# Row sums of a 16384 x 1024 array: a first load from the last group of rows, in place of a first block of 17 rows a partition

## The chip, the cores and the metric

The kernel runs on one core of one Trainium2 chip. The metric is the time of one execution on the device in microseconds (us), as the median of several runs. One further execution is taken with the hardware profiler; all durations of single instructions come from it.

## What is computed

```python
def setup_inputs():
    batch, seq, dim = 32, 512, 1024
    return {"x": np.random.randn(batch, seq, dim).astype(np.float32)}

def reference(x):
    return np.sum(x, axis=-1).astype(np.float32)
```

16384 rows of 1024 float32 are summed: 67.1 MB are read from HBM and 64 KB are written.

## The kernel before

**Tiles and loads.** The 16384 rows are shared out over 128 partitions, 128 rows each. The list `sizes` cuts them into eight blocks of 17, 15 and six times 16 rows a partition; within a block, partition p holds that many consecutive rows of `x`. So one partition's part of a load is a contiguous run, and neighbouring partitions begin 17, 15 or 16 rows (68, 60 or 64 KB) apart. `rows_from(j, n)` gives the n rows from the j-th on.

All loads are issued by SP, in program order, into tiles of the pool `in`, which has three buffers: a tile can be loaded anew once the sums of what it held are done. `rows(t, a, n, j, n_act, pairs)` (L208) issues one load of n rows a partition into tile `t` from place `a` on, and gives the sums of the last `n_act` of them to ScalarE (ACT) and of the others to VectorE (DVE).

**The three ways to sum a row.**
- `vec` (L172): one VectorE reduction over all its rows of the load at once.
- `halves` (L186), used with `pairs=True`: one VectorE instruction a row, which adds the two halves of the row and accumulates the result, and then a short read of the accumulator.
- `act` (L199): one ScalarE copy a row into PSUM with an accumulated sum, and a read of the accumulator. Its PSUM pool has four buffers, so each copy waits for the fourth before it, on the same engine.

All sums go into one SBUF tile, `sums`, 128 partitions x 128.

**The order of the loads.** Block 0 is loaded as 4 rows (`FIRST`) and 13 rows; then block 1 (15 rows) and blocks 2 to 6 (16 rows each). Block 6 is summed half by ACT, half by VectorE. The last block comes as 8 rows, 5 rows, 2 rows and one row in two pieces of 560 and 464 elements (L247, L248), so that little is left to sum when the last bytes arrive. The two pieces of the last row are summed by two `halves`; the first one's sum is put beside the second piece as a further element, and a small copy (`seen`) makes the second wait for it. The load of block 1 is held (`hold`, L230) until the first 4 rows are summed, and so are, behind it on SP, all the loads that follow.

**The stores.** On ACT's queue, behind its last copy and held until the load of 2 rows has landed, stand three stores: the sums of block 0 (17 a partition), of block 1 (15 a partition), and of blocks 2 to 6 (L252 for the first two, L254 for the third). The sums of the last block are stored by SP (L260).

**What is done to the finished program.** `issue_first_load_at_entry` moves the very first load in front of the meeting of all engines with which a program begins. `order_waits` puts, of several waits of one instruction, a given one first. `wait_for_the_store_at_the_clear` changes the end of the program (its instructions carry L286): there SP waits for everything that is still under way, all engines meet, GpSimd (POOL) clears the semaphores, and all meet again. The wait for SP's own last store is taken out of SP's waits and put behind POOL's clears, right before the last release; SP's waits for the ACT stores stay where they are.

Of the kernel before, what the change touches and what calls it, by code (L numbers as in the profile page):

```python
# [118 lines left out]
@with_exitstack  # L119
def kernel(  # L120
    ctx: ExitStack,
    tc: tile.TileContext,
    x: bass.AP,
    out: bass.AP,
):
    nc = tc.nc
    nc.at_finalize(issue_first_load_at_entry)
    nc.at_finalize(order_waits)
    nc.at_finalize(wait_for_the_store_at_the_clear)
    fp32 = mybir.dt.float32  # L130
    P = 128
    batch, seq, dim = x.shape
    rows = batch * seq
    J = rows // P
    BIG = 16

    sizes = [BIG + 1, BIG - 1] + [BIG] * (J // BIG - 2)  # L140
    begins = [sum(sizes[:k]) for k in range(len(sizes))]
    x_r = x.flatten_outer_dims()
    out_r = out.rearrange("b s -> (b s)")
    x_b = [
        x_r[a * P : (a + n) * P].rearrange("(p j) d -> p j d", p=P) for a, n in zip(begins, sizes)
    ]
    out_b = [out_r[a * P : (a + n) * P].rearrange("(p j) -> p j", p=P) for a, n in zip(begins, sizes)]
    out_g = out_r[2 * BIG * P :].rearrange("(g p j) -> p g j", p=P, j=BIG)

    def rows_from(j, n):  # L150
        k = max(k for k, a in enumerate(begins) if a <= j)
        j -= begins[k]
        return x_b[k][:, j : j + n, :]

    last = J // BIG - 1
    FIRST = 4
    pieces = (560, 464)

    with (
        tc.tile_pool(name="in", bufs=3) as inpool,
        tc.tile_pool(name="unread", bufs=4, space=bass.MemoryType.PSUM) as upool,
        tc.tile_pool(name="stage", bufs=1) as stpool,
        tc.manual_schedule(),
    ):
        sums = stpool.tile([P, J], fp32)
        seen = stpool.tile([P, 1], fp32)
        scratch = stpool.tile([P, pieces[1] // 2 + 1], fp32)

        def vec(dst, src):
            return nc.vector.tensor_reduce(  # L172
                out=dst, in_=src, axis=mybir.AxisListType.X, op=mybir.AluOpType.add
            )

        def hold(inst, until, reason):
            tc.add_manual_dep(
                inst.ins,
                until.ins.name,
                mybir.DependencyInfo(mybir.DependencyClass.Sync, mybir.DependencyReason.DATA),  # L180
                reason=reason,
            )

        def halves(dst, src, unread=None):
            n = src.shape[-1] // 2
            return nc.vector.tensor_tensor_reduce(  # L186
                out=src[:, :n] if unread is None else unread[:, :n],
                in0=src[:, :n],
                in1=src[:, n:],
                scale=1.0,  # L190
                scalar=0.0,
                op0=mybir.AluOpType.add,
                op1=mybir.AluOpType.add,
                accum_out=dst,
            )

        def act(dst, src, n):
            unread = upool.tile([P, dim], fp32)
            nc.scalar.activation(  # L199
                out=unread[:, :n],  # L200
                in_=src,
                func=mybir.ActivationFunctionType.Copy,
                accum_out=dst,
            )

        sums_of = []

        def rows(t, a, n, j, n_act, pairs=False):  # L208
            nv = n - n_act
            block = t[:, a * dim : (a + n) * dim].rearrange("p (n d) -> p n d", d=dim)  # L210
            load = nc.sync.dma_start(out=block, in_=rows_from(j, n))  # L211
            if pairs:
                for q in range(nv):
                    sums_of.append(halves(sums[:, j + q : j + q + 1], block[:, q, :]))
            else:
                sums_of.append(vec(sums[:, j : j + nv], block[:, :nv, :]))
            for q in range(nv, n):
                act(sums[:, j + q : j + q + 1], block[:, q, :], dim)
            return load

        for g in range(last):
            n, j = sizes[g], begins[g]
            t = inpool.tile([P, (BIG + 1) * dim], fp32)
            if g == 0:
                rows(t, 0, FIRST, j, 0)
                first = sums_of[-1]
                rows(t, FIRST, n - FIRST, j + FIRST, 0)
                continue
            load = rows(t, 0, n, j, BIG // 2 if g == last - 1 else 0)
            if g == 1:  # L230
                hold(load, first, "no descriptors of later loads while the first ones start")

        t = inpool.tile([P, (BIG + 1) * dim], fp32)
        j = last * BIG
        rows(t, 0, 8, j, 4)
        rows(t, 8, 5, j + 8, 2, pairs=True)
        two = rows(t, 13, 2, j + 13, 1, pairs=True)
        a = BIG - 1

        j += a
        c, width = pieces
        whole = t[:, a * dim + c : BIG * dim + 2]
        nc.vector.memset(whole[:, width + 1 :], 0.0)  # L245
        part = t[:, a * dim : a * dim + c]
        nc.sync.dma_start(out=part, in_=rows_from(j, 1)[:, 0, :c])  # L247
        nc.sync.dma_start(out=whole[:, 1 : width + 1], in_=rows_from(j, 1)[:, 0, c:])  # L248
        behind = "its packets come behind those of the loads"
        for k in range(2):  # L250
            mine = sums[:, begins[k] : begins[k] + sizes[k]]
            hold(nc.scalar.dma_start(out=out_b[k], in_=mine), two, behind)  # L252
        middle = sums[:, 2 * BIG : last * BIG].rearrange("p (g j) -> p g j", j=BIG)
        hold(nc.scalar.dma_start(out=out_g[:, : last - 2], in_=middle), two, behind)  # L254
        halves(whole[:, :1], part)


        nc.vector.tensor_copy(out=seen, in_=whole[:, :1])  # L258
        halves(sums[:, j : j + 1], whole, unread=scratch)
        nc.sync.dma_start(out=out_b[last], in_=sums[:, last * BIG :])  # L260


# [28 lines left out]
```

## Time and profile before

| | |
|---|---|
| time, median of 3 runs | 162.37 us (162.19 to 162.58) |
| time of the profiled execution | 162.19 us |
| its span in the profile | 160.33 us |
| loads, mean over the span | 419 GB/s |
| VectorE busy | 120.2 us |
| ScalarE busy | 17.3 us |
| packets of the stores from ACT's queue (q10) | 944 |

The span runs from the first to the last instruction of the program that the profiler saw; 1.86 us of the execution's time lie around it. Lines such as L172 are lines of the kernel above; SPq and ACTq are the queues on which SP and ACT issue transfers. In the list of the issues, the columns are the tensor written and read, the issuing engine, how many, the size, and the microseconds from issue to landing. In the other views, the last figures of an instruction's line are its shortest, median and longest duration in ns and the start of its first and last one in us.

### The profile page before, as it was taken

The page shows a single profiled execution, that of the slowest core. Times are in us where ns is not written, and L with a number is a line of the kernel's source. Part 1 is how long each engine was busy: PE and PEld are TensorE (multiplying, and loading weights), DVE is VectorE, ACT ScalarE, POOL GpSimd, SP SyncE. Part 2 cuts the span into 40 slices and gives each one's busy share as a digit, 9 for nine tenths or more (in the row PEclk, how much of TensorE's full clock was granted, in tenths as well). Part 3 has the DMA queues.
Part 4 walks back from the last instruction along what each step waited for, and adds up shares of the span by engine and source line. Part 5 has one row for each costly group of instructions (what it writes and reads, how often), then busy time and mean ns, then how long its engine had stood idle before and what let it go on. Part 6 is the DMA issues. An engine that isn't in the chain of part 4 may idle for free.

```text
span 160.3 us, 130 instructions
## 1 busy us (share of the span) xinstructions
DVE 120.2 (75%) x23; ACT 17.3 (11%) x31; POOL 0.2 (0%) x4
## 2 busy tenths in 40 slices
DVE  0190029992699938999499994999949999597944
ACT  3000000000000000000000000000000000596952
POOL 0000000000000000000000000000000000000000
DMA  7999999997996996997997998999969969999993
GB/s 258 478 425 425 425 458 491 491 399 337 523 507 278 523 507 278 523 458 327 523 441 343 523 425 360 523 392 392 523 294 491 523 278 507 392 392 430 414 400 81
DMA packets 2960, 67.18 MB, mean 419 GB/s; under 512 B 1296, under 2 KB 1424, under 8 KB 1552
## 3 DMA queue, kind: packets, MB, share of 16 engines
q1 hardware_dynamic: 2016, 67.12, 97.4%
q10 hardware_dynamic: 944, 0.06, 0.4%
HBM read 67.11 MB, written 0.07 MB: 419 GB/s over the span
## 4 chain that ended last, share of the span: by engine, by line
DMA 73%; DVE 24%; SPq 1%; issue 0%; DVEq 0%
DMA t<-in_x_dram 73%; DVE sums L172 24%; SPq L211 1%; DVE t L186 0%; DVE scratch L186 0%; DVE seen L258 0%; DVEq L286 0%
## 5 line engine op out<-in xcount | busy, mean ns | idle before, releaser
L172 DVE TENSOR_REDUCE sums<-t 128x16 f32<-128x16384 f32 (+4 forms) x9 | 116.6, 12954 | 35.6 <-DMA t<-in_x_dram 35.6
L199 ACT ACTIVATE unread<-t 128x1024 f32<-128x1024 f32 x15 | 15.2, 1012 | 139.5 <-DMA t<-in_x_dram 139.5
L186 DVE CUSTOM_DVE_ANT_0 t<-t 128x512 f32<-128x512 f32 (+1 forms) x5 | 3.1, 642 | 2.3 <-DMA t<-in_x_dram 2.3
L199 ACT ACTIVATION_READ_ACCUMULATOR unread<-t 128x1 f32 x15 | 2.8, 187 | 0.0
L199 ACT ACT_TABLE_LOAD x1 | 1.3, 1283 | 0.8 <-PEq L275 0.8
L186 DVE DVE_READ_ACCUMULATOR2_ANT sums<- 128x1 f32 x5 | 0.4, 83 | 0.0
L186 DVE CUSTOM_DVE_ANT_0 scratch<-t 128x233 f32<-128x233 f32 x1 | 0.4, 403 | 0.0
L258 DVE COPY seen<-t 128x1 f32<-128x1 f32 x1 | 0.2, 154 | 0.0
L275 POOL MEMSET const-bfloat16-1.0<- 128x1 bf16 x1 | 0.1, 101 | 0.0
L275 POOL MEMSET const-uint8-127<- 128x1 uint8 x1 | 0.1, 101 | 0.0
L275 POOL MEMSET const-float32-0.0<- 128x1 f32 x1 | 0.1, 98 | 0.2 <-issue 0.2
L275 POOL MEMSET const-float32-1.0<- 128x1 f32 x1 | 0.1, 98 | 0.0
L186 DVE DVE_READ_ACCUMULATOR2_ANT t<- 128x1 f32 x1 | 0.1, 83 | 0.0
L245 DVE MEMSET t<- 128x1 f32 x1 | 0.1, 59 | 0.0
## 6 DMA issues: line engine op xcount, KB each, us to landing
t<-in_x_dram SPq DMA_DIRECT2D x1, 7680.0 KB, 29.4
t<-in_x_dram SPq DMA_DIRECT2D x1, 6656.0 KB, 22.4
t<-in_x_dram SPq DMA_DIRECT2D x1, 4096.0 KB, 31.1
t<-in_x_dram SPq DMA_DIRECT2D x1, 2560.0 KB, 36.9
t<-in_x_dram SPq DMA_DIRECT2D x1, 2048.0 KB, 7.4
t<-in_x_dram SPq DMA_DIRECT2D x1, 1024.0 KB, 38.9
t<-in_x_dram SPq DMA_DIRECT2D x1, 280.0 KB, 39.2
t<-in_x_dram SPq DMA_DIRECT2D x1, 232.0 KB, 39.2
```

Of the source, the lines that this page charges most:

```text
L172: return nc.vector.tensor_reduce(out=dst, in_=src, axis=mybir.AxisListType.X, op=mybir.AluOpType.add)
L186: return nc.vector.tensor_tensor_reduce(out=src[:, :n] if unread is None else unread[:, :n], in0=src[:, :n], in1=src[:, n:], scale=1.0, sc ...
L199: nc.scalar.activation(out=unread[:, :n], in_=src, func=mybir.ActivationFunctionType.Copy, accum_out=dst,)
L211: load = nc.sync.dma_start(out=block, in_=rows_from(j, n))
L245: nc.vector.memset(whole[:, width + 1 :], 0.0)
L258: nc.vector.tensor_copy(out=seen, in_=whole[:, :1])
L275: nc = _bacc.Bacc("TRN2", target_bir_lowering=False, num_devices=1)
```

## The change

The blocks of 17 and 15 rows go; there are eight groups of 16 rows a partition, all 64 KB apart from partition to partition. The first load is now of seven rows of the last group (`FIRST = 7`), into a tile of its own, summed by one reduction. Then seven whole groups are loaded by one load each. The last of these is summed by VectorE as nine single rows (`pairs=True`) and by ACT as seven. Then the remaining nine rows of the last group follow as 6 rows (four on VectorE, two on ACT), 2 rows (one each) and the same two pieces of one row. The load of group 1 is held until the first seven rows are summed. The three stores from ACT become one, of the sums of groups 0 to 6, held as they were until the load of 2 rows has landed. What is done to the finished program is the same.

```diff
-    sizes = [BIG + 1, BIG - 1] + [BIG] * (J // BIG - 2)
-    begins = [sum(sizes[:k]) for k in range(len(sizes))]
-    x_r = x.flatten_outer_dims()
-    out_r = out.rearrange("b s -> (b s)")
-    x_b = [
-        x_r[a * P : (a + n) * P].rearrange("(p j) d -> p j d", p=P) for a, n in zip(begins, sizes)
-    ]
-    out_b = [out_r[a * P : (a + n) * P].rearrange("(p j) -> p j", p=P) for a, n in zip(begins, sizes)]
-    out_g = out_r[2 * BIG * P :].rearrange("(g p j) -> p g j", p=P, j=BIG)
+    x_g = x.flatten_outer_dims().rearrange("(g p j) d -> g p j d", p=P, j=BIG)
+    out_v = out.rearrange("b s -> (b s)").rearrange("(g p j) -> p g j", p=P, j=BIG)
 
     def rows_from(j, n):
-        k = max(k for k, a in enumerate(begins) if a <= j)
-        j -= begins[k]
-        return x_b[k][:, j : j + n, :]
+        return x_g[j // BIG, :, j % BIG : j % BIG + n, :]
...
-    FIRST = 4
+    FIRST = 7
...
+        def store(eng, g0, g1):
+            return eng.dma_start(
+                out=out_v[:, g0:g1],
+                in_=sums[:, g0 * BIG : g1 * BIG].rearrange("p (g j) -> p g j", j=BIG),
+            )
+        j = last * BIG
+        t = inpool.tile([P, BIG * dim + 4], fp32)
+        rows(t, 0, FIRST, j, 0)
+        first = sums_of[-1]
         for g in range(last):
-            n, j = sizes[g], begins[g]
-            t = inpool.tile([P, (BIG + 1) * dim], fp32)
-            if g == 0:
-                rows(t, 0, FIRST, j, 0)
-                first = sums_of[-1]
-                rows(t, FIRST, n - FIRST, j + FIRST, 0)
-                continue
-            load = rows(t, 0, n, j, BIG // 2 if g == last - 1 else 0)
+            t = inpool.tile([P, BIG * dim + 4], fp32)
+            if g < last - 1:
+                load = rows(t, 0, BIG, g * BIG, 0)
+            else:
+                rows(t, 0, BIG, g * BIG, 7, pairs=True)
             if g == 1:
                 hold(load, first, "no descriptors of later loads while the first ones start")
 
-        t = inpool.tile([P, (BIG + 1) * dim], fp32)
-        j = last * BIG
-        rows(t, 0, 8, j, 4)
-        rows(t, 8, 5, j + 8, 2, pairs=True)
-        two = rows(t, 13, 2, j + 13, 1, pairs=True)
+        t = inpool.tile([P, BIG * dim + 4], fp32)
+        rows(t, FIRST, 6, j + FIRST, 2, pairs=True)
+        two = rows(t, FIRST + 6, 2, j + FIRST + 6, 1, pairs=True)
         a = BIG - 1
...
-        behind = "its packets come behind those of the loads"
-        for k in range(2):
-            mine = sums[:, begins[k] : begins[k] + sizes[k]]
-            hold(nc.scalar.dma_start(out=out_b[k], in_=mine), two, behind)
-        middle = sums[:, 2 * BIG : last * BIG].rearrange("p (g j) -> p g j", j=BIG)
-        hold(nc.scalar.dma_start(out=out_g[:, : last - 2], in_=middle), two, behind)
+        hold(store(nc.scalar, 0, last), two, "its packets come behind those of the loads")
         halves(whole[:, :1], part)
...
-        nc.sync.dma_start(out=out_b[last], in_=sums[:, last * BIG :])
+        store(nc.sync, last, last + 1)
```

## The prediction

> **What bounds the kernel now.** I read the page's shares first, then the queues, then the chain of waits. Each fence below is one view.
>
> ```profile
> DVE 120.2 (75%) x23; ACT 17.3 (11%) x31; POOL 0.2 (0%) x4
> ...
> q1 hardware_dynamic: 2016, 67.12, 97.4%
> ```
>
> No compute engine is near full, while the load queue q1 keeps the 16 DMA engines busy for 97.4% of the span: the kernel is one stream of loads with a start before it and an end behind it. The chain in order of time shows where the stream stops deciding:
>
> ```profile
> 117.98 39.15 DMA t<-in_x_dram
> 157.13 0.03 issue
> 157.16 0.47 DVE t L186 x2
> 157.63 0.02 issue
> 157.65 0.15 DVE seen L258
> 157.80 0.33 DVE scratch L186
> 158.13 0.01 DVEq L286
> ```
>
> The stream (but for its last piece) is in at 157.13 and VectorE ends at 158.13, yet the span is 160.3. So 2.2 us lie behind the last arithmetic. For these I read the issues of the stores, SP's own waits, and the end sequence (L286) cut into two windows, 158.5 to 159.45 and 159.9 to 160.33:
>
> ```profile
> out_dram<-sums ACTq DMA_DIRECT2D x1, 40.0 KB, 1.9
> out_dram<-sums ACTq DMA_DIRECT2D x1, 8.5 KB, 1.5
> ...
> out_dram<-sums SPq DMA_DIRECT2D x1, 8.0 KB, 1.4
> ```
> ```profile
> SPq L286 <- DMA out_dram<-sums: 0.7, 1, 0.7
> ```
> ```profile
> L286 SPq EVENT_SEMAPHORE x4: 28/28/678, 158.6 to 159.4; - x4
> ```
> ```profile
> L286 POOLq EVENT_SEMAPHORE x3: 17/17/17, 159.9 to 160.3; - x3
> ```
>
> The timeline puts the four stores' issues at 156.48 and, 0.49 later, 156.97 (ACT, 17 and 15 sums a partition), at 157.40 (ACT, 40 KB) and at 158.16 (SP, the last 8 KB):
>
> ```profile
> 157.40 0.44 ACTq L254 DMA_DIRECT2D out_dram<-sums  x1
> ...
> 158.16 0.35 SPq L260 DMA_DIRECT2D out_dram<-sums  x1
> ```
>
> The 40 KB store lands at about 157.40 + 1.95 = 159.35, the last one at 158.16 + 1.42 = 159.58. SP stands 678 ns on the former, until 159.37. The rest of the end (two meetings of all engines, two semaphore clears) then takes from 159.37 to 160.33, 0.96 us, and the last store is waited for only in POOL's wait near 160.2, where it has been in for 0.6 us. **So the end is set by the third ACT store, not by the last store**, and the three waits of 17 ns in the last fence show that nothing else is waited for there.
>
> **The change, part by part.**
>
> *The loads.* Starts of the VectorE reductions follow landings by 0.02 us: 7.45, 23.16, 41.32, 60.66, 80.01, 99.37, 118.71, 138.07, 147.78, 153.92, 156.42. The gaps are 15.71 us for 13 rows, 18.16 for 15, 19.35 for 16, 9.71 for 8, 6.14 for 5, 2.50 for 2. A line through 16 and 2 rows is (19.35 - 2.50) / 14 = 1.204 us a row and 0.093 a load; it gives 15.74, 18.15, 9.72 and 6.11 for the others. The first load of 4 rows lands at 7.43, 2.52 more than its 4.91 by that line. The new loads are 7, seven times 16, 6, 2 and the two pieces, 12 in place of 13, so the stream ends 0.09 earlier: 7 rows at 7.45 + 3 x 1.204 = 11.06, the seventh group at 11.06 + 7 x 19.35 = 146.51, 6 rows (7.32) at 153.83, 2 rows at 156.33, against 156.42.
>
> *Buffers and SP's queue.* The load of the second group waits for the first reduction, which at 8.69 / 8 = 1.08 us a row takes 7.6 us and ends at 18.6 (before: 11.87). Behind it on SP stand all later loads. The queue holds 7 + 16 rows until 30.4, so nothing runs dry; without the whole group behind the first load it would cost 18.6 - 11.0 = 7.6 us. Each later load waits for the reduction two groups before the landing one: group 3 for the reduction of group 0, 30.4 + 17.2 = 47.6, with group 2 queued until 69.1. The four last loads wait for group 4 (107.8 + 17.2 = 125.0) with group 6 queued until 146.5. Over 20 us of cover each time; SP issues in 0.33 to 0.46 us each.
>
> *VectorE and ACT at the tail.* Group 6 gives VectorE 9 rows as pairs (0.615 us a row, from 153.92, 154.54, 155.15) in place of 8 at 1.08: done by 146.5 + 5.6 = 152.1, before the 6 rows come at 153.83. ACT does 7 rows in 7.4 us (8 took 8.4): 153.9, 0.1 behind the 6 rows. Its two rows end at 156.0, before 156.33: free. VectorE now has 4 rows there where it had 3: 153.83 + 4 x 0.615 + 0.08 = 156.37, 0.04 after the landing of the 2 rows. So of the 0.09 gained, 0.05 reach the last reduction, which ends at 158.08, and the last store is issued at 158.11. Each further 0.1 of delay on VectorE there would move the end by 0.1.
>
> *The stores.* Two ACT issues of 0.39 us go. One store of 7 groups, 7 x 128 runs of 64 B, waits for the 2 rows, for VectorE's and ACT's sums of group 6 (152.1 and 153.9, long past), and is issued where the first was, 0.06 behind the landing: about 156.4. Behind it on ACT stands only the end. No row shows such a store. 128 runs took 1.5, 640 took 1.9, so 512 more cost 0.4 and 896 should take 2.1: landed at 158.5. The far bound is 1.9 x 896 / 640 = 2.7: 159.1. SP comes to its end waits at 158.56 - 0.05 = 158.5 and to the next ones every 0.07, so at 2.1 the store holds it for 0.07 at most, against 0.68. I take 2.1, since both rows show a large fixed part. Then POOL comes to its last wait 0.66 to 0.7 earlier, near 159.55, and now meets the last store's landing at 158.11 + 1.42 = 159.53. Both bounds agree: the end moves from 160.33 to about 159.65, **0.68 earlier, of which 0.05 comes from the loads and 0.63 from the store**.
>
> *The start.* Before, partition p of the first block begins 17 rows (68 KB) after its neighbour, the second block 15 rows; now every load has a pitch of 64 KB, and the first one starts all DMA engines from rest at that pitch. No row has this. In the running stream the pitch costs nothing: 15.71 / 13 = 1.208 us a row at 68 KB against 19.35 / 16 = 1.209 at 64 KB. From rest, the first load's 2.52 us hold 0.9 before the first packet and a slow first packet on each engine: 1.1 us on the mean of the stretch from 0.9 to 2.0 (18.9 us of engine time for 17 packets), against 0.61 for the following ones. The low bound is a gain of 0.1 (larger packets). The high bound is that the first packet, now 28 KB or 1.07 us long, takes twice as long on the last engine: +1.07. I take 0, by the row of the same pitch.
>
> A rule speaks against this part. The Trainium skill, "DMA: Bandwidth & Descriptors", section "Latency and other measured facts", reports that copies whose partitions lie a large power of two apart lose rate (207 GB/s at 512 KiB, 103 at 4 MiB, 214 again with 4 KiB of padding), and its cause there is only inferred. The trace agrees so far as it goes that 64 KB apart is harmless while the stream runs. By the rule's mildest case, an estimate from that page, the first load would lose 3%, about 0.3 us of its 8.5, and the sum would be a gain of 0.4 in place of 0.7.
>
> *Sum.* The profiled execution took 162.19 for a span of 160.33. 162.19 - 0.68 = 161.51. It is the lowest of the three runs, 0.18 under the median, so the median becomes 162.37 - 0.68 = **161.7**.
>
> **The rivals.** 0.2% is about what a measurement of this kernel can tell from no change: 0.32 us.
>
> 1. *The start at 64 KB pitch loses more than the end gains.* For it: the first packets are the only ones in the trace that run slower than the ports, so the engines do collide at the start, and the engines' first rows now lie whole multiples of 64 KB apart. Against it: the issue itself spreads the first packets over 0.9 to 1.9 us. The whole stream would shift, since nothing later can catch up with it. Price at its bound: -0.68 + 1.07 = +0.39, 162.8. It decides for slower from 1.0 us of extra start; a second packet as slow would give 163.8.
> 2. *The start takes back about half.* A loss of 0.36 to 1.0 leaves -0.32 to +0.32; at 0.6, 162.3.
> 3. *The merged store is slow.* At the far bound it lands at 159.1, SP leaves its wait at 159.13, and as this wait now stands one place earlier in the row, 0.07 + 0.96 follow: 160.16, a gain of 0.17, 162.2. For it: 896 runs in one issue. Against it: the fixed 1.4 us of the 8 KB store.
> 4. *The end gains, but less, because the last store lands late,* in the 1.5 to 1.7 of the small ACT stores: the gain is 0.4 to 0.6, still faster, 161.9. It is part of the forecast's own range, 161.4 to 162.0.
>
> **How the numbers follow.** Faster by 0.68 or somewhat less: 0.48. Rival 1: 0.34, since the bound is only a guess from one packet and no row shows the start. Rivals 2 and 3 together: 0.18. These are the chances of faster, slower and the same. The time is the likeliest one, 161.7. The range goes down to 161.3 (0.1 gained at the start, the other 0.3 run-to-run: the three runs spread over 0.39) and up to 162.9, just past rival 1's bound; beyond that is left perhaps 0.15.
>
> **What would show it.** Right: the first reduction starts near 11.06 and the first whole group's near 30.4; groups 19.35 apart; the 2 rows' reduction near 156.37; one ACT store of 56 KB landing in about 2.1; no long wait of SP on a store in the end; POOL's clears near 159.3. Rival 1 shows as a first reduction at 12 or later, with all starts behind it shifted as much and groups still 19.35 apart. Rival 3 shows as a landing over 2.5 and SP's wait on it. The prediction is wrong if the groups' distance grows beyond 19.35: then the pitch costs in the stream too, and seven groups multiply it.

## The result and the profile after

| | before | after |
|---|---|---|
| median of 6 runs each | 162.33 us (162.13 to 162.58) | 161.58 us (161.40 to 161.66) |
| profiled execution | 162.19 us | 161.59 us |
| its span | 160.33 us | 159.7 us |

The ratio is 0.9952, with a 95% interval of 0.9940 to 0.9965: 0.75 us less on the medians, 0.60 in the two profiled executions. The prediction was 161.7, by a gain of 0.68.

The page of the changed kernel, its share of the load queue:

```profile
q1 hardware_dynamic: 1872, 67.12, 97.7%
```

Its timeline, the landings as VectorE sees them (start and length in us, line, tiles, then the idle time before it and what ended it):

```profile
11.07 7.62 DVE L161 TENSOR_REDUCE sums<-t 128x7 f32<-128x7168 f32 x1 [11.07 <-DMA t<-in_x_dram]
30.40 17.22 DVE L161 TENSOR_REDUCE sums<-t 128x16 f32<-128x16384 f32 x1 [11.71 <-DMA t<-in_x_dram]
...
127.18 17.22 DVE L161 TENSOR_REDUCE sums<-t 128x16 f32<-128x16384 f32 x1 [2.14 <-DMA t<-in_x_dram]
...
146.62 0.69 DVE L175 CUSTOM_DVE_ANT_0 t<-t 128x512 f32<-128x512 f32 x1 [2.23 <-DMA t<-in_x_dram]
...
156.41 0.69 DVE L175 CUSTOM_DVE_ANT_0 t<-t 128x512 f32<-128x512 f32 x1
156.50 0.41 ACTq L211 DMA_DIRECT2D out_dram<-sums  x1
...
157.16 0.45 DVE L175 CUSTOM_DVE_ANT_0 t<-t 128x280 f32<-128x280 f32 x1
...
158.17 0.35 SPq L211 DMA_DIRECT2D out_dram<-sums  x1
```

The last store is issued at 158.17, where it was issued before at 158.16. Up to there the two executions are level: the loads gave nothing in this one. The gain lies in what follows. Its issues of stores (size in KB, us to landing) and SP's own waits:

```profile
out_dram<-sums ACTq DMA_DIRECT2D x1, 56.0 KB, 2.1
out_dram<-sums SPq DMA_DIRECT2D x1, 8.0 KB, 1.4
```
```profile
SPq L200 <- DMA t<-in_x_dram: 17.9, 5, 10.9
SPq L276 <- PEq L276: 0.7, 2, 0.5
```

The row of SP waiting 0.7 us for `out_dram<-sums` is gone; the row on PEq, one of the meetings, was there before with the same numbers. The end sequence between 158.5 and 159.45, and from the kernel before the clears of POOL, in the window from 159.9 to 160.33:

```profile
L276 SPq EVENT_SEMAPHORE  x5: 17/28/28, 158.6 to 159.1; - x5
...
L276 POOLq EVENT_SEMAPHORE_RANGE_CLEAR  x2: 46/58/71, 159.3 to 159.4; - x2
```
```profile
L286 POOLq EVENT_SEMAPHORE_RANGE_CLEAR  x2: 44/59/74, 160.0 to 160.1; - x2
```

None of SP's semaphore instructions there is longer than 28 ns, where one was 678, and POOL clears at 159.3 to 159.4, where it cleared at 160.0 to 160.1. The one ACT store, issued at 156.50, landed at 158.63, just before SP came to its wait at 158.65. The last store landed at 159.60, and POOL's last wait, which is for it, ended 0.02 us later; before, that store had been in for 0.64 us by then.

### The profile page after: what moved, and what is told of

It reads as the page before. It is cut to its first block, busy times and chain, and to the rows that moved or that the text cites. A ratio compares the mean times of both kernels' runs of the same rounds, so it can differ in the third digit from the quotient of the medians.

```text
span 159.7 us, 134 instructions
## 1 busy us (share of the span) xinstructions
DVE 120.7 (76%) x41; ACT 11.9 (7%) x21; POOL 0.2 (0%) x4
## 4 chain that ended last, share of the span: by engine, by line
DMA 71%; DVE 27%; SPq 0%; issue 0%; DVEq 0%
DMA t<-in_x_dram 71%; DVE sums L161 26%; SPq L200 0%; DVE t L175 0%; DVE scratch L175 0%; DVE seen L248 0%; DVEq L276 0%
## 5 line engine op out<-in xcount | busy, mean ns | idle before, releaser
L161 DVE TENSOR_REDUCE sums<-t 128x16 f32<-128x16384 f32 (+1 forms) x7 | 110.9, 15848 | 33.5 <-DMA t<-in_x_dram 33.5
L188 ACT ACTIVATE unread<-t 128x1024 f32<-128x1024 f32 x10 | 10.1, 1013 | 144.9 <-DMA t<-in_x_dram 144.9
L175 DVE CUSTOM_DVE_ANT_0 t<-t 128x512 f32<-128x512 f32 (+1 forms) x15 | 9.2, 672 | 4.0 <-DMA t<-in_x_dram 3.9
L188 ACT ACTIVATION_READ_ACCUMULATOR unread<-t 128x1 f32 x10 | 1.9, 187 | 0.0
L175 DVE DVE_READ_ACCUMULATOR2_ANT sums<- 128x1 f32 x15 | 1.2, 82 | 0.0
```

What stands on the lines that cost most here:

```text
L161: return nc.vector.tensor_reduce(out=dst, in_=src, axis=mybir.AxisListType.X, op=mybir.AluOpType.add)
L175: return nc.vector.tensor_tensor_reduce(out=src[:, :n] if unread is None else unread[:, :n], in0=src[:, :n], in1=src[:, n:], scale=1.0, sc ...
L188: nc.scalar.activation(out=unread[:, :n], in_=src, func=mybir.ActivationFunctionType.Copy, accum_out=dst,)
```

## The experiments

Each was timed in five or more runs beside the kernel before on the same chip; "before" is that median. The profile quoted is of one execution. "Store theory" in the expectations is the reading of the prediction: the end waits for the last of the ACT stores.

**Three stores again, in the changed kernel.**

```diff
-        hold(store(nc.scalar, 0, last), two, "its packets come behind those of the loads")
+        for g0, g1 in ((0, 1), (1, 2), (2, last)):
+            hold(store(nc.scalar, g0, g1), two, "its packets come behind those of the loads")
```

> The changed kernel with its one ACT store split again into groups 0, 1 and 2 to 6. Store theory: the third store is issued 0.9 us after the first and lands near 159.35, SP stands on it for about 0.65 us, and the time goes back by 0.6, to 162.2, level with the kernel before. Rival, that the gain lies in the loads: the time stays at 161.6.

Measured 162.20 against 162.25 before, ratio 1.0003 (0.9995 to 1.0012). With its loads untouched, the changed kernel has lost the whole gain. SP's waits and ACT's issues there:

```profile
SPq L277 <- DMA out_dram<-sums: 0.7, 1, 0.7
```
```profile
156.35 0.91 ACTq L211 DMA_DIRECT2D out_dram<-sums  x2
...
157.35 0.39 ACTq L211 DMA_DIRECT2D out_dram<-sums  x1
...
158.03 0.35 SPq L211 DMA_DIRECT2D out_dram<-sums  x1
```

The wait is back, and the third issue comes 1.0 us after the first.

**Two stores, in the changed kernel.** The same edit with `((0, 1), (1, last))`.

> The changed kernel with its ACT store as two, of group 0 and of groups 1 to 6. Store theory, in which the end follows the landing of the last ACT store: the second is issued 0.49 after the first and lands 2.1 later, near 159.1; SP comes to its wait for it near 158.65 to 158.7, stands 0.35 to 0.45 us, and the time is 161.9 to 162.0, between one store (161.6) and three (162.2). Rival, that only the number of runs or bytes in flight counts: 161.6, as with one.

Measured 161.85 against 162.22, ratio 0.9982 (0.9973 to 0.9991), between the other two. SP's wait:

```profile
SPq L277 <- DMA out_dram<-sums: 0.4, 1, 0.4
```

So one, two and three stores give waits of 0, 0.4 and 0.7 us and times of 161.6, 161.85 and 162.2. The time follows the wait, not the bytes, which are the same each time. The step from one to two costs less than the wait: 0.25 on the medians, and 0.36 if one counts from the issue of the last store to the end of the span (1.92 against 1.57 us). With one store POOL waits some 0.04 us for the last store instead; the rest of the difference lies in the streams.

**The small stores early, in the kernel before.** The loads stay as they were; the stores of blocks 0 and 1 are moved out of the tail.

```diff
+            if g == 4:
+                for k in range(2):
+                    nc.scalar.dma_start(out=out_b[k], in_=sums[:, begins[k] : begins[k] + sizes[k]])
...
-        for k in range(2):
-            mine = sums[:, begins[k] : begins[k] + sizes[k]]
-            hold(nc.scalar.dma_start(out=out_b[k], in_=mine), two, behind)
```

(The semaphore of the last store comes to lie at the edge of the cleared range, so that POOL needs one clear there, not two. This brings nothing: POOL's last wait ends 0.02 us after the landing of the last store here too.)

> The kernel before with its loads untouched (17, 15 and 16 rows, first load of 4), but the stores of blocks 0 and 1 issued by ACT as soon as their sums are done, near 57 us, long before its copies; only the 40 KB store stays behind the 2-row load. Store theory: it is issued 0.9 earlier, lands at 158.4 to 158.5, SP does not wait for it, and the time falls by 0.5 to 0.7, to 161.6 to 161.8; the 256 small runs cost the stream at most 16 x 0.01 = 0.16 us. Rival, that the loads of the change bring the gain: 162.3.

Measured 161.66 against 162.22, ratio 0.9968 (0.9956 to 0.9980). This is the gain of the change with none of its loads: the changed kernel measured 161.60 on the same chip. The two small stores went out at 37.26 and 57.54. The wait of SP on a store is gone from its profile, and the early stores show something else:

```profile
out_dram<-sums ACTq DMA_DIRECT2D x1, 40.0 KB, 1.9
out_dram<-sums ACTq DMA_DIRECT2D x1, 8.5 KB, 23.7
out_dram<-sums ACTq DMA_DIRECT2D x1, 7.5 KB, 22.8
```

In the stream, a store that takes 1.5 us at its end takes 23.7 to land. It costs nothing there, since nobody waits for it before the end.

**The large store first, in the kernel before.** The 40 KB store is issued ahead of the two small ones.

```diff
-        for k in range(2):
-            mine = sums[:, begins[k] : begins[k] + sizes[k]]
-            hold(nc.scalar.dma_start(out=out_b[k], in_=mine), two, behind)
         middle = sums[:, 2 * BIG : last * BIG].rearrange("p (g j) -> p g j", j=BIG)
         hold(nc.scalar.dma_start(out=out_g[:, : last - 2], in_=middle), two, behind)
+        for k in range(2):
+            mine = sums[:, begins[k] : begins[k] + sizes[k]]
+            hold(nc.scalar.dma_start(out=out_b[k], in_=mine), two, behind)
```

> The kernel before with its 40 KB store issued as the first of the three ACT stores. Store theory: the 40 KB land at 156.5 + 1.95 = 158.4, and the last of the three is now the 7.5 KB store, issued near 157.4 and landing 1.5 to 1.7 later, at 158.9 to 159.1; SP waits 0.25 to 0.4 us in place of 0.68 and the time falls by 0.25 to 0.45, to about 162.0. Rival, that the last store or the loads set the end: no change, 162.3.

Measured 162.15 against 162.29, ratio 0.9994 (0.9985 to 1.0003): the expectation of 0.25 to 0.45 failed. The timeline and SP's wait say why:

```profile
156.88 0.42 ACTq L251 DMA_DIRECT2D out_dram<-sums  x1
157.35 0.58 ACTq L254 DMA_DIRECT2D out_dram<-sums  x1
...
157.96 0.45 ACTq L254 DMA_DIRECT2D out_dram<-sums  x1
```
```profile
SPq L286 <- DMA out_dram<-sums: 0.6, 1, 0.6
```

(This execution's stream was some 0.4 us later than the others'.) The issues behind the large store took 0.58 and 0.45 us in place of 0.39 and 0.44, so the third came 1.08 us after the first, not 0.92, and the small store then took 1.7. The wait shrank by 0.1 only. What costs is to be the third issue; which store is third matters little.

**The pitch alone, in the kernel before.**

```diff
-    sizes = [BIG + 1, BIG - 1] + [BIG] * (J // BIG - 2)
+    sizes = [BIG] * (J // BIG)
```

> The kernel before with 16 rows in every block, so that all partitions lie 64 KB apart; still a first load of 4 rows and three ACT stores. If the pitch at the start costs nothing: 162.3, the first reduction at 7.45. Rival, that 17 and 15 rows spread the first packets and help: the first reduction at 7.8 or later and the time up by as much, 162.7 or more.

Measured 162.13 against 162.25, ratio 1.000 (0.999 to 1.001). Its timeline:

```profile
7.27 4.42 DVE L172 TENSOR_REDUCE sums<-t 128x4 f32<-128x4096 f32 x1 [7.27 <-DMA t<-in_x_dram]
```

The first four rows were in at 7.27, not later than the 7.45 of the kernel before. A start at a pitch of 64 KB costs nothing against 68 KB. If anything it helps: the three profiles with this first load at 64 KB, here and in the next two runs with it, have 7.27, 7.12 and 7.34; the three at 68 KB have 7.45 (before), 7.49 (small stores early) and 7.37 (large store first).

**The pitch and one store, in the kernel before**, twice, the second time beside the changed kernel.

```diff
-    sizes = [BIG + 1, BIG - 1] + [BIG] * (J // BIG - 2)
+    sizes = [BIG] * (J // BIG)
...
+        groups = sums[:, : last * BIG].rearrange("p (g j) -> p g j", j=BIG)
+        out_v = out_r.rearrange("(g p j) -> p g j", p=P, j=BIG)
+        hold(nc.scalar.dma_start(out=out_v[:, :last], in_=groups), two, behind)
```

> The same as the kernel before with 16 rows in every block, and its three ACT stores as one of groups 0 to 6; 13 loads as before, first load of 4 rows. Store theory: 161.6 to 161.7, the whole gain of the change without the seven rows first and without the load less. Rival, that the seven rows first or the load less bring it: 162.3.

Measured 161.66 against 162.25, ratio 0.9969 (0.9957 to 0.9981).

> The changed kernel once more, beside the next one on the same chip: 161.6.

> The kernel before with 16 rows in every block and one ACT store, beside the changed kernel on the same chip. If the seven rows first and the load less bring the 0.09 of the per-load row: 0.05 to 0.1 above the changed kernel. Rival, that they bring nothing because a first packet of 28 KB starts later than one of 16 KB (first reductions at 11.07 and 7.12, 2.5 and 2.2 us more than their rows cost): level with it or below.

On one chip, against 162.22 before: the changed kernel 161.60, ratio 0.9968 (0.9956 to 0.9981); this one 161.41, ratio 0.9957 (0.9945 to 0.9968). The intervals overlap, and the 0.05 to 0.1 that the changed kernel was expected to be ahead did not show. The seven rows first, the load less and the sums in pairs bring nothing that can be measured; uniform groups are needed only so that one store can hold all of them.

**A pitch of 512 KB, in the changed kernel.**

```diff
-    x_g = x.flatten_outer_dims().rearrange("(g p j) d -> g p j d", p=P, j=BIG)
-    out_v = out.rearrange("b s -> (b s)").rearrange("(g p j) -> p g j", p=P, j=BIG)
+    x_g = x.flatten_outer_dims().rearrange("(p g j) d -> g p j d", p=P, j=BIG)
+    out_v = out.rearrange("b s -> (b s)").rearrange("(p g j) -> p g j", p=P, j=BIG)
```

> The changed kernel with each partition's 128 rows consecutive, so that every load has its partitions 512 KB apart; the ACT store then has 128 runs of 448 B in place of 896 of 64 B. If the pitch is harmless for runs of this length: 161.5 to 161.6, the store landing 1.5 after its issue, groups 19.35 apart. If a power of two of 512 KB costs the 3% that the Trainium skill's page DMA: Bandwidth & Descriptors has for it: groups near 19.9 apart and 165 to 166.

Measured 162.07 against 162.25, ratio 0.9993 (0.9982 to 1.0003): 0.5 above the changed kernel, and neither of the two expectations. Its timeline:

```profile
11.38 7.62 DVE L161 TENSOR_REDUCE sums<-t 128x7 f32<-128x7168 f32 x1 [11.38 <-DMA t<-in_x_dram]
30.72 17.22 DVE L161 TENSOR_REDUCE sums<-t 128x16 f32<-128x16384 f32 x1 [11.72 <-DMA t<-in_x_dram]
50.06 17.22 DVE L161 TENSOR_REDUCE sums<-t 128x16 f32<-128x16384 f32 x1 [2.12 <-DMA t<-in_x_dram]
69.74 17.22 DVE L161 TENSOR_REDUCE sums<-t 128x16 f32<-128x16384 f32 x1 [2.46 <-DMA t<-in_x_dram]
89.08 17.22 DVE L161 TENSOR_REDUCE sums<-t 128x16 f32<-128x16384 f32 x1 [2.12 <-DMA t<-in_x_dram]
```

The start is 0.31 later than in the changed kernel, whose loads started their first reduction at 10.99 to 11.10 in five profiles; one group took 19.68, and the others are 19.34 apart as ever. So the running stream does not lose 3%, which would be 0.6 a group, but a start from rest at this pitch did lose something in this one profile. Whether the one long group belongs to the pitch is open, since this is one profile.

**The store one load earlier, in the changed kernel.**

```diff
-        rows(t, FIRST, 6, j + FIRST, 2, pairs=True)
+        six = rows(t, FIRST, 6, j + FIRST, 2, pairs=True)
+        hold(store(nc.scalar, 0, last), six, "its packets come among those of the last loads")
...
-        hold(store(nc.scalar, 0, last), two, "its packets come behind those of the loads")
```

> The changed kernel with its ACT store held only until the 6 rows have landed, and issued ahead of the ACT copy of the 2-row load. Theory that the store has left the path: nothing is gained by landing it earlier, and its 896 runs now go through the DMA engines among the last loads, 57 packets of 0.01 us on each, so the stream ends 0.4 to 0.6 later: 162.0 to 162.2. Rival, that the store still holds the end: 161.3 or less.

Measured 161.62 against 162.29, ratio 0.9960 (0.9946 to 0.9973): nothing gained, as the theory said, but nothing measurable lost either, against its 0.4 to 0.6. In its profile (timeline and issues)

```profile
153.99 0.42 ACTq L211 DMA_DIRECT2D out_dram<-sums  x1
```
```profile
out_dram<-sums ACTq DMA_DIRECT2D x1, 56.0 KB, 4.3
```

the store lands at 158.3, hardly earlier than the 158.6 of the changed kernel. In the trace its packets went through from 156.65 to 157.60, behind all loads that were queued before it but the last piece, and among the packets of that piece. That piece landed 0.72 us after the piece before it, against 0.57 in the changed kernel: the store cost the stream about 0.15 us, not 0.4 to 0.6. From the issue of the last store to the end of the span it is 1.56 us, as in the changed kernel (1.57), though the ACT store is now in 0.3 us before SP comes to its wait: the landing of this store is off the path.

## Why the prediction was right

What brought the gain is the merged store. The first load from the last group, which the title names, brought nothing that can be measured.

- *What sets the end.* Right, and shown from both sides: three stores put back in the changed kernel cost 0.6, and two stores taken out of the old tail gain 0.56, each with the loads untouched. The profiles show it without the scatter of the streams, in the time from the issue of the last store to the end of the span (the span to two decimals is the execution's time less the 1.86 us around it). It is 2.15 to 2.17 us in the three profiles with three stores in the old order, 2.05 with the large one first, 1.92 with two, and 1.54 to 1.57 in all seven in which SP waits for no ACT store. In these seven, POOL's last wait ends 0.02 us after the last store has landed, and would have ended 0.02 to 0.08 us earlier without it: POOL is through 0.045 us after its drain where the store has long been in. So the last store is the next in line, as the prediction said, by very little.
- *The merged store.* Predicted to take 2.1 and land at 158.5; it took 2.1 and landed at about 158.6. The bound of 2.7 was far off, since the cost is mostly fixed: 1.5 us for 128 runs, 1.9 for 640, 2.1 for 896.
- *The size of the gain at the end.* Predicted 0.63, from 160.33 to 159.65 with the loads' share. The span ended at 159.73, and the last-store issue was at 158.17 in place of 158.11: the end sequence itself became 0.60 shorter. The forecast of 0.68 lies between the gains of the two sets of runs, 0.75 here and 0.62 in the repetition.
- *The start.* Predicted 11.06, measured 11.07. That the 64 KB pitch costs nothing was right, and the experiment with the pitch alone shows it. That the number fits so closely is partly luck. The sum took the same 2.5 us before the first rows' own time for a first load of 7 rows as for one of 4. At the same pitch of 64 KB the loads of 4 rows came at 7.27, 7.12 and 7.34, some 2.2 to 2.4 above 4 x 1.204 + 0.093, and the loads of 7 rows at 11.07 and 11.02, 2.5 above theirs. So the larger first load gives back 0.1 to 0.3, against the low bound's gain of 0.1 for larger packets, and this cancels the 0.2 by which a start at 64 KB was earlier than one at 68. (The stretch from 0.9 to 2.0 us, read in the prediction as 17 packets, held 16, one an engine: 1.18 us on their mean.)
- *One load less, 0.09 and 0.05 of it at the end.* The term can't be told from zero: with three stores put back, the new loads measured 162.20 against 162.25, at a ratio of 1.0003. In the profiled execution it was lost on the way: by 107.81 all stood as worked out, but the next two groups took 19.37 and 19.44, and the tail began at 146.62, not 146.51. In the repetition it began at 146.46 and the last store was issued at 158.02. The kernel with 13 loads, a 64 KB pitch and one store was level all the same, which fits its earlier start.
- *Buffers and the tail of VectorE.* Right: the groups came 19.33 to 19.36 apart up to 107.81, so SP's waits for buffers never left the load queue empty, and four rows in pairs on VectorE ended in time for the 2 rows at 156.41 (predicted 156.37).
- *The rivals.* The start at 64 KB pitch (chance 0.34) costs nothing. A loss at the start was seen at 512 KB, 0.3 us, a third of the rival's bound. For that pitch, the rule that the prediction quoted from the Trainium skill ("DMA: Bandwidth & Descriptors", section "Latency and other measured facts"), measured there with 16 KiB a partition, does not show in the stream of this kernel, where each run is 64 KB long: an estimate by its 3% would be 19.9 a group, and five of the six distances are 19.34 or 19.35.

## What to carry to other kernels

When a kernel's last arithmetic ends well before its span, read the end as a stage of its own: which of the waits there is long, and for which transfer. Issues of one engine stand in a row, 0.4 to 0.6 us each here, so a transfer at the tail costs by its place in the row before it costs by its bytes; merge such stores, or issue all but the last while the stream still hides them. Then look for the next wait in line: here it stood 0.04 us behind, and moving the merged store earlier still brought nothing. And a layout that stands in the way of merging has to earn what the extra issues cost.

## What the runs showed that was not expected

- A store issued from ACT into the running stream lands late by a regular amount: 23.7 us for 128 runs of 68 B, eight a DMA engine. The queues in that profile from 44.9 to 47.3 us (packets, MB, share), about as long as one load packet of 64 KB takes (19.35 / 8 = 2.42 us):

```profile
q1 hardware_dynamic: 16, 1.05, 100.8%
q10 hardware_dynamic: 16, 0.00, 0.5%
```

Each of the 16 engines moved one packet of the loads (q1) and one of the store (q10), and so it did from 42.5 to 44.9 and from 47.3 to 49.7. So the eight packets of the store on an engine stood 2.42 us apart, 7 x 2.42 = 17.0 us from the first to the last. The first ones went 5.3 to 6.1 us after the issue, and the landing came 0.6 us after the last. How long a store's first packet waits (2.7 us in the run with the store one load earlier) was not looked into.
- In the run with the large store first, the issue right behind it (640 runs) took 0.58 us; right behind a store of 128 runs ACT's issues took 0.39 to 0.49 us. The 0.58 was seen once.
- The stream itself varies: a group of 16 rows mostly takes 19.32 to 19.37, but in some executions single groups take 19.4 to 19.7, at places that differ between executions. Over a run this comes to as much as 0.5 us, more than the 0.09 that was weighed for a load less; what causes it was not looked into.
